# One early product, a few weight buffers and the order of some sums, stores and reads in a hybrid decoder layer

## The chip, the cores and the metric

The kernel runs on one core of one Trainium2 chip. The metric is the device time of one execution in microseconds; the time of a kernel is the median of its runs. The core has five engines with an instruction stream each: TensorE (PE, with its weight loads shown as PEld), VectorE (DVE), ScalarE (ACT), GpSimd (POOL) and SyncE (SP). Each executes its own stream in order. Transfers are issued by the instruction streams, here by SP (its hardware queue) and by POOL (its software queue), and land some microseconds later.

## What is computed

One layer of a hybrid decoder: 1024 tokens and 16 meta tokens, model width 1024, feed-forward width 4096, all float32. The part that matters here is the last line but one:

```python
u = rmsnorm(h, g_pre_mix[l])
z = u @ w_in[l]
...
mix = jnp.concatenate([attn, rec], axis=-1) @ w_out[l]
h = h + rmsnorm(mix, g_post_mix[l])
u = rmsnorm(h, g_pre_ffn[l])
f = jnp.square(jax.nn.relu(u @ w_ff1[l])) @ w_ff2[l]
h = h + rmsnorm(f, g_post_ffn[l])
```

## The kernel before

**Stages.** The in-projection, attention and recurrence take the first 280 us or so, the output projection and its norm run to about 330 us, the first feed-forward matrix (FF1) to about 640 us, the second (FF2) to the end. The change lies in the last stages of the out-projection, in FF1 and in FF2.

**Numbers in two parts.** Every float32 operand is split in a high and a low part (L94 to L101): ACT casts the value (L96) and DVE subtracts the cast from the value (L99). `mm3` (L123) then multiplies high by high (L125), high weights by the low part of the other operand (L126) and low weights by its high part (L127). One `product` (L999) is four of these over the contraction: 12 matmuls of 128x512.

**Seven products in place of eight.** FF1 and FF2 are each worked as a two by two block product in the manner of Strassen: sums of weight blocks times sums of operand blocks, so that seven products do instead of eight, at the price of sums on DVE. FF1 runs over 16 chunks p of 256 columns of `w_ff1`. Its weights come as two loads, r0 (upper half of the contraction) and r1 (lower half). `prep_a(p)` (L1012) issues both, makes the sums in place (four DVE operations of L989), splits what is needed, and stores the summed r1 in `s_dram[p]` on POOL's queue (L1034) for a later loop. The operand sums are t2, t3 and t4; their splits are `ot2`, `ot3`, `ot4`. The splits of t4 are made during the first loop by `t_rest` (L1153) and written to a scratch in DRAM, `t4_dram`, with four stores on SP's queue (L1165), since `ot4` is needed only some 130 us later.

**Buffers.** All slabs come by tag, with a fixed number of buffers each (L55): raw 2, ws 4 (weight splits), a 16, b 17, c 8, d 4, e 2. A load into a buffer waits until its last user is done. r1 of chunks 2 to 5 takes "a" buffers (L1015), which held the projection's splits and later hold results of the chunks; the other chunks take "d".

**Early products.** Before the main loop, while the last tiles of the norm are still worked on, PE computes the products with ready operands: `p1` (L1095) of chunks 0 to 3 and `p2` (L1100) of chunks 0 to 3, `p2` into the PSUM bank "pt", from where DVE adds it to block "11" (L1103). Then the first loop (L1168): for each chunk the second product (with `ot2`, L1173), its copy by ACT (L1174), `p1` of chunk p + 2, and the third product (with `ot3`, L1177), its copy (L1178). Second and third accumulate in the same bank, so the third waits for the copy. For p = 0 there is no `p1` between them, since chunk 2 is done early.

**The second and third loop of FF1.** The second loop (L1197) works the stored sums. Behind it `ot4` is read back from `t4_dram` in four reads on SP's queue (L1214 to L1217): the high halves of both tiles, then the low halves. The third loop runs over the chunks in the order `third` (L1294). Its first step, n = 0, uses `product_by_parts` (L1219), which does the four matmuls high by high, then low weights by high, then high weights by low; so the low halves come into play last. The other steps use `product`.

**FF2.** 56 steps, 7 products by 8 parts (`PLAN`, L1232). `fetch_2` (L1249) loads the weights of a step: one load on SP (L1261), and where a sum of two blocks is wanted, either a second transfer on POOL that adds into the first buffer while landing (L1258, for two of three parts) or a second load, and the sum is made on DVE by `prep_2` (L1270). `prep_2` splits them in "ws" buffers (L1274).

**The order.** Within these dependences a scheduler decides, by simulated times, in which order each engine's stream has its instructions. An extra order without a wait is put in by `behind(name, ins)` (L106): `ins` comes after the instruction of that name in the schedule. `w_low` holds the name of the last low split (L1274); only for i = 6 is the next sum put behind it (L1272).

Of the kernel before, what the change touches and what calls it, by code (L numbers as in the profile page):

```python
# [16 lines left out]
P = 128  # L17
# [20 lines left out]
def hybrid_layer(  # L38
# [6 lines left out]
    nc = tc.nc  # L45
# [23 lines left out]
    def f32(ap):  # L69
        return ap.bitcast(F32)  # L70
# [51 lines left out]

    def mm3(dst, lhs, rhs, start, stop):  # L123
        (lh, ll), (rh, rl) = lhs, rhs
        nc.tensor.matmul(dst, lh, rh, start=start, stop=False, skip_group_check=True)  # L125
        nc.tensor.matmul(dst, lh, rl, start=False, stop=False, skip_group_check=True)  # L126
        last_mm[0] = nc.tensor.matmul(  # L127
            dst, ll, rh, start=False, stop=stop, skip_group_check=True
        ).ins.name
# [868 lines left out]

    def product(acc, w, op, first):  # L999
        wh, wl = w  # L1000
        for kc in range(4):
            hh, ll = op[kc // 2]
            mm3(
                acc, (wh[:, kc, :], wl[:, kc, :]), (hh[:, kc % 2, :], ll[:, kc % 2, :]),
                first and kc == 0, kc == 3,
            )
# [5 lines left out]
    def prep_a(p, late=None):  # L1012
        r0 = slot("raw", [P, 4, 256])
        w1_load(r0, 0, p, 0, 2)
        r1 = slot("a" if 2 <= p < 6 else "d", [P, 4, 256])  # L1015
        w1_load(r1, 1, p, 0, 2)
# [82 lines left out]

    def p2(p, w):  # L1100
        y2 = bank("pt")
        product(y2, w, b21, True)
        nc.vector.tensor_tensor(block("11", p), y2, block("11", p), op=ALU.add)  # L1103
# [41 lines left out]
    a12_early.update(early(1, 2, pair("a", ESH)))  # L1145
    for p in range(2, 4):
        p2(p, a12_early[p])
    ot3 = [pair("b", [P, 2, 512]) for _ in range(2)]
# [5 lines left out]
    def t_rest(k):  # L1154
        i = k % 2
        if k < 2:
            behind(mark[0], combine(u2f[1][i], u2f[1][i], u2f[0][i], ALU.subtract))
        elif k < 4:
            behind(mark[0], combine(t2[i], u2f[0][2 + i], t2[i], ALU.subtract))
        else:  # L1160
            hl = pair("a", [P, 2, 512])
            late = mark[0]
            behind(late, split(*hl, t2[i]))
            for n in range(2):
                nc.sync.dma_start(t4_dram[:, n, 2 * i : 2 * i + 2, :], f32(hl[n]))  # L1165

    raw_b, raw_c = {}, {}
    for p in range(16):  # L1168
# [4 lines left out]
        product(ya[p], wa[p][1], ot2, False)  # L1173
        nc.scalar.copy(block("12", p), ya[p])  # L1174
        if 4 <= p + 2 < 16:
            p1(p + 2, wa[p + 2][0])
# [37 lines left out]
    ot4 = [pair("b", [P, 2, 512]) for _ in range(2)]  # L1214
    for n in range(2):
        for i in range(2):
            nc.sync.dma_start(f32(ot4[i][n]), t4_dram[:, n, 2 * i : 2 * i + 2, :])  # L1217

    def product_by_parts(acc, w, op):  # L1219
        for k, (a, b) in enumerate(((0, 0), (1, 0), (0, 1))):  # L1220
            for kc in range(4):
                nc.tensor.matmul(
                    acc, w[a][:, kc, :], op[kc // 2][b][:, kc % 2, :],
                    start=k == 0 and kc == 0, stop=k == 2 and kc == 3,
                    skip_group_check=True,
                )

# [37 lines left out]
    def prep_2(n, tag="ws"):  # L1265
# [21 lines left out]

    w_low = [None]

# [4 lines left out]
    for n, p in enumerate(third):  # L1294
# [205 lines left out]
```

## Time and the profile before

| What | Value |
|---|---|
| Time, median of 3 runs | 957.42 us (956.74 to 957.98) |
| The profiled execution's own time | 957.43 us |
| Its span | 955.7 us |
| DVE busy | 659.3 us |
| ACT busy | 504.3 us |
| POOL busy | 124.6 us |
| HBM read / written | 109.93 MB / 18.87 MB |
| Loads raw<-w_ff, issue to landing, median | 4.4 us |
| Reads b<-t_dram, issue to landing, median | 5.9 us |

The profile is of one execution. A row of the timeline gives the start, the duration, the engine, the line in the code, the operation, output<-inputs by the program's names (`ps_acc`, `ps_s`, `ps_pt`, `ps_o` are PSUM banks; `ws` and `e` weight splits, `b` operand splits), the shape and, in brackets, how long the engine was idle before it and what ended that. Several like instructions in a row are shown as one, with xN. "SPq" is a transfer at SP's queue; its bar is the issue, the landing comes later. A wait row gives the waiting instruction, the releaser, total, count and longest. A stretch row gives start:end, its length, the busy time with the number of instructions that touch it, the granted clock, the DMA share and GB/s. PE's matmuls overlap, each runs longer than the distance to the next, so that a lost fraction of a microsecond shows as a distance between two starts, and not always as an idle time.

### The profile page before, as it was taken

The numbers are of one execution on the slowest core, as the hardware profiler recorded it, in microseconds if no ns is written. First come the engines' busy times: TensorE is split into PE (matmuls) and PEld (weight loads), VectorE is DVE, ScalarE is ACT, GpSimd is POOL, SyncE is SP. The second block draws the span as 40 slices with busy tenths as digits, with TensorE's granted clock in tenths as the row PEclk, the third lists the DMA queues.
The fourth block names the chain that finished last, engine by engine and source line by source line (L and its number), as shares of the span: only waits on it lengthen the run. The fifth ranks groups of instructions, "written<-read, shape, count | busy, mean of one in ns | idle before, by whom it ended". The sixth has DMA issues, their size and how long they took to land.

```text
span 955.7 us, 12406 instructions
## 1 busy us (share of the span) xinstructions
PE 944.6 (99%) x4728; PEld 789.8 (83%) x4728; DVE 659.3 (69%) x845; ACT 504.3 (53%) x854; POOL 124.6 (13%) x184
## 2 busy tenths in 40 slices
PE   9999999999999999999999999999999999999996
PEld 8999999877888877888888878888888788888885
DVE  6567997779866776665644465476576776779883
ACT  7537766478645554443555575563433343446441
POOL 4102563420020100000000000000111100001201
PEclk9999999999999999999999999999999999999999
DMA  8221011104235466675522353324767765547934
GB/s 271 57 67 23 24 45 46 45 23 134 77 120 177 133 220 198 197 259 160 184 102 90 110 192 119 109 92 129 176 171 182 198 219 178 197 133 199 241 67 89
DMA packets 88200, 130.22 MB, mean 136 GB/s; under 512 B 13702, under 2 KB 52630, under 8 KB 88140
## 3 DMA queue, kind: packets, MB, share of 16 engines
q1 hardware_dynamic: 79548, 106.54, 34.3%
q0 software_dynamic: 8160, 21.57, 10.9%
q10 hardware_dynamic: 432, 1.31, 0.4%
q8 instruction: 37, 0.61, 0.3%
q14 instruction: 23, 0.19, 0.1%
HBM read 109.93 MB, written 18.87 MB: 135 GB/s over the span
## 4 chain that ended last, share of the span: by engine, by line
PE 91%; DVE 3%; ACT 2%; SPq 1%; POOL 1%; DMA 1%; issue 1%; DVEq 0%; ACTq 0%; POOLq 0%
PE ps_acc L125 11%; PE ps_acc L126 11%; PE ps_acc L127 11%; PE ps_pt L125 7%; PE ps_pt L126 7%; PE ps_pt L127 6%; PE ps_s L127 6%; PE ps_s L126 6%; PE ps_s L125 6%; PE ps_o L127 5%; PE ps_o L126 5%; PE ps_o L125 5%; PE ps_o L684 1%; POOL c L673 1%; ACT c L82 1%; DMA c<-in_x_dram 1%
## 5 line engine op out<-in xcount | busy, mean ns | idle before, releaser
L96 ACT CAST ws<-raw 128x1024 fp32r<-128x1024 f32 (+1 forms) x68 | 69.6, 1024 | 121.6 <-PE ps_o L126 46.9
L99 DVE TENSOR_TENSOR ws<-raw,ws 128x1024 fp32r<-128x1024 f32 (+1 forms) x69 | 82.4, 1195 | 53.8 <-ACT ws L96 52.8
L125 PE MATMUL ps_acc<-a,ws 128*128 128x256 f32 (+2 forms) x256 | 85.8, 335 | 0.0
L127 PE MATMUL ps_acc<-a,ws 128*128 128x256 f32 (+2 forms) x256 | 85.2, 333 | 0.0
L126 PE MATMUL ps_acc<-a,ws 128*128 128x256 f32 (+2 forms) x256 | 85.1, 333 | 0.0
L99 DVE TENSOR_TENSOR b<-b,b 128x1024 fp32r<-128x1024 f32 (+2 forms) x50 | 58.9, 1179 | 25.9 <-PE ps_o L126 17.1
L96 ACT CAST ws<-e 128x1024 fp32r<-128x1024 f32 x41 | 42.9, 1046 | 64.0 <-PE ps_o L126 40.2
L96 ACT CAST b<-b 128x1024 fp32r<-128x1024 f32 (+2 forms) x49 | 50.0, 1019 | 45.8 <-DVE b L989 40.2
L99 DVE TENSOR_TENSOR ws<-e,ws 128x1024 fp32r<-128x1024 f32 x41 | 50.1, 1223 | 24.2 <-ACT ws L96 24.0
L673 POOL TENSOR_SCALAR_AFFINE_SELECT c<-c 128x512 fp32r<-128x512 f32 x64 | 52.1, 834 | 70.3 <-ACT c L96 60.8
L125 PEld LDWEIGHTS ps_acc<-a,ws 128*128 128x128 f32 x256 | 48.3, 189 | 4.6 <-issue 0.2
L127 PEld LDWEIGHTS ps_acc<-a,ws 128*128 128x128 f32 x256 | 48.2, 188 | 4.5
L126 PEld LDWEIGHTS ps_acc<-a,ws 128*128 128x128 f32 x256 | 48.1, 188 | 4.4 <-issue 0.4
L126 PE MATMUL ps_acc<-ws,b 128*128 128x512 f32 (+1 forms) x120 | 46.2, 385 | 0.9 <-DVE ws L99 0.9
L125 PE MATMUL ps_acc<-ws,b 128*128 128x512 f32 (+1 forms) x120 | 46.2, 386 | 0.0
L127 PE MATMUL ps_acc<-ws,b 128*128 128x512 f32 (+1 forms) x120 | 46.2, 385 | 0.0
L125 PE MATMUL ps_pt<-ws,b 128*128 128x512 f32 x112 | 44.4, 396 | 0.0
L126 PE MATMUL ps_pt<-ws,b 128*128 128x512 f32 x112 | 44.1, 394 | 0.0
L127 PE MATMUL ps_pt<-ws,b 128*128 128x512 f32 x112 | 44.0, 393 | 0.0
L125 PE MATMUL ps_s<-ws,b 128*128 128x512 f32 x110 | 43.4, 395 | 0.0
L127 PE MATMUL ps_s<-ws,b 128*128 128x512 f32 x110 | 43.3, 394 | 0.0
L126 PE MATMUL ps_s<-ws,b 128*128 128x512 f32 x110 | 43.3, 393 | 0.0
(414 smaller groups left out, 2662.7 us busy)
## 6 DMA issues: line engine op xcount, KB each, us to landing
raw<-in_w_ff_dram SPq DMA_DIRECT2D x61, 512.0 KB, 4.4
e<-in_w_ff_dram SPq DMA_DIRECT2D x45, 512.0 KB, 3.4
d<-in_w_ff_dram SPq DMA_DIRECT2D x12, 512.0 KB
s_dram<-d POOLq DMA_DIRECT2D x12, 512.0 KB, 4.1
c<-in_x_dram SPq DMA_DIRECT2D x8, 512.0 KB, 3.5
raw<-in_w_in_dram SPq DMA_DIRECT2D x8, 512.0 KB
d<-in_x_dram SPq DMA_DIRECT2D x8, 512.0 KB, 3.2
out_dram<-raw SPq DMA_DIRECT2D x8, 512.0 KB
```

What stands on the lines that cost most here:

```text
L82: ins = nc.scalar.activation(*args, **kwargs).ins
L96: nc.scalar.copy(hi, src)
L99: low = nc.vector.tensor_tensor(lo, src, f32(hi), op=ALU.subtract).ins
L125: nc.tensor.matmul(dst, lh, rh, start=start, stop=False, skip_group_check=True)
L126: nc.tensor.matmul(dst, lh, rl, start=False, stop=False, skip_group_check=True)
L127: last_mm[0] = nc.tensor.matmul(dst, ll, rh, start=False, stop=stop, skip_group_check=True).ins.name
L673: nc.gpsimd.affine_select(out=p_[:, :, s], in_=f32(p_[:, :, 0]), pattern=[[0, 4], [g, P]], compare_op=op, fill=0.0, base=0, channel_multip ...
L684: nc.tensor.matmul(po[:, oc : oc + n], v, p_[:, pc : pc + n], start=first and k == 0, stop=last and k == 1, skip_group_check=True,)
```

## The change

It has five parts.

- `p2` of chunk 3 moves from the early products into the first loop, for p = 0, between the copy of the second product and the third product. A new argument `after` puts its first matmul behind the last matmul of the second product.
- r1 of chunks 2 to 13, not 2 to 5, takes "a" buffers.
- The four stores to `t4_dram` go out on POOL's queue.
- `ot4` is read tile by tile (high and low of the first, then of the second), and the step n = 0 uses `product` like the others.
- In FF2 the sum of step n, for i < 6 and n > 1, is put behind the low split of step n − 2.

With them the scheduler arrives at other orders. On DVE they differ between about 340 and 460 us and between 675 and 760 us: a low split of weights comes ahead of the sum of a later step, and in FF1 the sum for chunk 14 comes ahead of the low split of chunk 13. On POOL and SP four pairs of adding transfers and loads of FF2 are exchanged, and the loads of r1 of chunks 14 and 15 go out right after that of chunk 6. On PE only `p2` of chunk 3 changes its place and the 12 matmuls of the step n = 0 change their order.

```diff
-    def mm3(dst, lhs, rhs, start, stop):
+    def mm3(dst, lhs, rhs, start, stop, after=None):
         (lh, ll), (rh, rl) = lhs, rhs
-        nc.tensor.matmul(dst, lh, rh, start=start, stop=False, skip_group_check=True)
+        ins = nc.tensor.matmul(
+            dst, lh, rh, start=start, stop=False, skip_group_check=True
+        ).ins
+        if after:
+            behind(after, ins)
...
-    def product(acc, w, op, first):
+    def product(acc, w, op, first, after=None):
...
-                first and kc == 0, kc == 3,
+                first and kc == 0, kc == 3, after if kc == 0 else None,
...
-        r1 = slot("a" if 2 <= p < 6 else "d", [P, 4, 256])
+        r1 = slot("a" if 2 <= p < 14 else "d", [P, 4, 256])
...
-    def p2(p, w):
+    def p2(p, w, after=None):
         y2 = bank("pt")
-        product(y2, w, b21, True)
+        product(y2, w, b21, True, after)
...
-    for p in range(2, 4):
-        p2(p, a12_early[p])
+    p2(2, a12_early[2])
...
-                nc.sync.dma_start(t4_dram[:, n, 2 * i : 2 * i + 2, :], f32(hl[n]))
+                nc.gpsimd.dma_start(t4_dram[:, n, 2 * i : 2 * i + 2, :], f32(hl[n]))
...
         nc.scalar.copy(block("12", p), ya[p])
+        if p == 0:
+            p2(3, a12_early[3], last_mm[0])
...
-    for n in range(2):
-        for i in range(2):
+    for i in range(2):
+        for n in range(2):
             nc.sync.dma_start(f32(ot4[i][n]), t4_dram[:, n, 2 * i : 2 * i + 2, :])
...
             ins = combine(raws[0], raws[0], raws[1], wx[2])
             if i == 6:
                 behind(w_low[0], ins)
+            elif n > 1:
+                behind(w_lows[n - 2], ins)
         wh, wl = pair(tag, [P, 2, 512])
-        w_low[0] = split(wh, wl, raws[0]).name
+        w_low[0] = w_lows[n] = split(wh, wl, raws[0]).name
...
-        if n == 0:
-            product_by_parts(y4, wc[p][1], ot4)
-        else:
-            product(y4, wc[p][1], ot4, True)
+        product(y4, wc[p][1], ot4, True)
```

More of the change, by code (lines that the diff above doesn't have):

```diff
@@ L1214, in hybrid_layer @@
     ot4 = [pair("b", [P, 2, 512]) for _ in range(2)]
-    for n in range(2):
-        for i in range(2):
+    for i in range(2):
+        for n in range(2):
             nc.sync.dma_start(f32(ot4[i][n]), t4_dram[:, n, 2 * i : 2 * i + 2, :])
[L1219 to L1226, printed above, removed]
     w2v = w_ff2.rearrange("(q s a p) (b c) -> q a b p s c", s=2, a=2, p=P, b=2)
@@ L1286, in hybrid_layer @@
     ready, raw_2 = {}, {}
-    w_low = [None]
+    w_low, w_lows = [None], {}
     load_root(squared)
```

## The prediction

> **What bounds the kernel now.** I began with the page's head, for the span and the busy shares, then read what TensorE (PE) and its weight loads (PEld) waited for, and then PE's busy time in stretches.
>
> ```profile
> span 955.7 us, 12406 instructions
> PE 944.6 (99%) x4728; PEld 789.8 (83%) x4728; DVE 659.3 (69%) x845; ACT 504.3 (53%) x854; POOL 124.6 (13%) x184
> ...
> PE ps_acc L303 <- DVE base_e L557: 1.5, 1, 1.5
> ...
> 341.00:367.00 26.00, 25.32 (x107) 1.00 0.63 207
> 367.00:559.00 192.00, 192.00 (x829) 1.00 0.49 162
> 559.00:564.00 5.00, 5.00 (x22) 1.00 0.72 248
> 564.00:741.00 177.00, 177.00 (x766) 1.00 0.51 139
> 741.00:744.00 3.00, 2.06 (x10) 1.00 0.36 110
> 744.00:942.00 198.00, 198.00 (x885) 1.00 0.59 171
> ```
>
> PE is the bound: 944.6 of 955.7 us, at a granted clock of 1.00 in all six stretches. The long stretches give its pace: 192.00 us over 829 matmuls is 0.2316 us from start to start. The change adds and removes no matmul, so it can move the end only by opening or closing gaps in that row. The largest wait, 1.5 us on base_e, belongs to L303 and L557, in the attention part, which the change leaves alone. Of the 601 us from 341 to 942, PE idles in two stretches only, 26.00 − 25.32 = 0.68 us and 3.00 − 2.06 = 0.94 us; some smaller losses, in which a matmul starts late without an idle row, come below. **All there is to win is some 3 us, 0.3% of the time**; 0.2%, about what a measurement of this kernel can tell from no change, is 1.9 us. VectorE (DVE, 69%) and the DMA queues matter where one result is late.
>
> **Part A: the last early product is moved (p2 of chunk 3, 12 matmuls).**
>
> ```profile
> 341.34 0.40 PE L126 MATMUL ps_pt<-b,a 128*128 128x512 f32 x1
> ...
> 346.66 0.40 PE L127 MATMUL ps_acc<-b,e 128*128 128x512 f32 x1
> 347.73 0.50 PE L125 MATMUL ps_acc<-b,ws 128*128 128x512 f32 x1 [0.68 <-ACT a L1174]
> 348.07 0.39 PE L126 MATMUL ps_acc<-b,ws 128*128 128x512 f32 x1
> ...
> 362.24 0.39 PE L126 MATMUL ps_s<-b,e 128*128 128x512 f32 x1
> 362.53 0.51 PE L127 MATMUL ps_s<-b,e 128*128 128x512 f32 x1
> ...
> 340.65 0.76 DVE L99 TENSOR_TENSOR b<-a,b 128x256 fp32r<-128x256 f32 x2 [0.33 <-ACT b L96]
> 350.99 1.29 DVE L99 TENSOR_TENSOR e<-raw,e 128x512 fp32r<-128x512 f32 x2
> 357.80 0.69 DVE L989 TENSOR_TENSOR a<-raw,a 128x512 f32<-128x512 f32 x1 [4.92 <-DMA raw<-in_w_ff_dram]
> ```
>
> The second product of chunk 0 (L1173) ends with the matmul that starts at 346.66. The third (L1177) reuses its PSUM bank and waits for the copy of L1174 until 347.73; the next matmul starts at 348.07. Two steps of 0.23 took 1.41 us, so the stall costs 1.41 − 0.46 = 0.95. After the change the 12 matmuls of p2(3), 12 × 0.2316 = 2.8 us, stand between the two, and a copy of 0.6 us hides behind them. The second product then starts where p2(3) stood, at about 341.4. It needs its operand's last low half at its eighth matmul, near 343.0; the low splits that started at 340.65 are over by 341.4 (0.76 us for two), or 342.6 if DVE does the sum of p2(2) ahead of the last: in time. The third product starts near 346.9 instead of 347.73.
>
> What is late next? In the same stretch four smaller starts are late, each read in the same manner from pairs of rows such as 362.24 and 362.53 (0.29 instead of 0.23, with a long next step): near 350.7, 351.7, 362.5 and 365.5, together about 0.7. The stretch's row agrees: of its 107 matmuls two only reach in at its ends (each runs 0.39, 0.23 apart), and 26.00 − 105 × 0.2316 = 1.7 = 0.95 + 0.7. They wait for splits of weight sums. In front of those, PE comes 0.95 earlier, and DVE, rid of the p2(3) sum at this place, 0.6 earlier: the low split at 350.99 stays just in time, and I leave 0.4 of loss there. The two late starts at 362 and 365 come from the chunk whose load DVE awaited until 357.80; that load goes out with a buffer freed sooner, and I take those two as closed. A: 0.95 + 0.7 − 0.4, rounded, **a gain of 1.2** (bounds 0 and 1.65).
>
> **Parts B and C: r1 of chunks 6 to 13 in "a" buffers.** The buffers hold nothing else then, so no load waits for them. But "d" becomes free for chunks 14 and 15, whose loads the SP queue issues far ahead, and DVE's order changes with it.
>
> ```profile
> 362.51 0.37 SPq L986 DMA_DIRECT2D raw<-in_w_ff_dram  x1
> 367.44 0.68 DVE L99 TENSOR_TENSOR e<-raw,e 128x512 fp32r<-128x512 f32 x1
> a<-in_w_ff_dram SPq DMA_DIRECT2D x4, 512.0 KB, 7.3
> ...
> 432.72 0.69 DVE L989 TENSOR_TENSOR d<-raw,d 128x512 f32<-128x512 f32 x1 [1.19 <-DMA d<-in_w_ff_dram]
> 435.14 0.69 DVE L99 TENSOR_TENSOR e<-raw,e 128x512 fp32r<-128x512 f32 x1
> 438.65 1.23 DVE L99 TENSOR_TENSOR ws<-raw,ws 128x1024 fp32r<-128x1024 f32 x1 [2.83 <-ACT ws L96]
> ...
> 440.82 0.39 PE L127 MATMUL ps_acc<-b,ws 128*128 128x512 f32 x1
> DMA to landing us min/median/max: 5.7/5.7/5.7
> ```
>
> B: the load of chunk 5's r1, which in the old order was long there, now goes out with its r0, as the second of five in a row, near 361.8 (the r0 load at 362.51, about 0.8 earlier with PE). DVE sums it ahead of the low split that stood at 367.44, and PE needs that split about 370.0. The "a" loads took 7.3 us as a median, which gives 369.1 plus four operations, 371.5: 1.5 late. A landing after 5 us gives 369.2, in time. It is second of the burst, and the r0 at its side is nearer to 5: I take 0.3 lost (bounds 0 and 1.5).
>
> C: near 438, DVE's sum for chunk 14, which stood after it before, now comes ahead of chunk 13's low split (438.65), and must wait for chunk 14's r0. That load follows the low split of 435.14, which itself moves up by some 1.6 us (it no longer stands behind all four sums that began with the wait of 432.72), less what PE gains: out at 434.2. With the 5.7 us that two raw loads of this stretch took, it lands at 439.9, the sum ends at 440.6 and the split at 441.9, where PE wants it at 440.82: 1.05 lost. If it lands before 437.9 the split isn't late at all. Half: **0.5 lost**.
>
> **The t4 stores on POOL's queue.** Four issues leave SP and stand between POOL's stores of L1034. Nothing waits for them before the ot4 reads over 100 us later, nor does PE wait for those stores. Price 0; were the cover gone, one POOL issue would cost about half a microsecond.
>
> ```profile
> 435.62 0.53 POOL L1034 DMA_DIRECT2D s_dram<-d  x1 [10.02 <-DVE d L989]
> 559.94 3.21 PE L1222 MATMUL ps_pt<-b,ws 128*128 128x512 f32 x12
> 562.41 0.30 PEld L1222 LDWEIGHTS ps_pt<-b,ws 128*128 128x128 f32 x2 [0.43 <-DMA b<-t_dram]
> 552.95 2.85 SPq L1217 DMA_DIRECT2D b<-t_dram  x4
> ```
>
> **Part D: ot4 in plain product order.** The four reads start at 552.95. Before, the step begins at 559.94 with eight matmuls on the operand's high halves; the fourth read, the low half of the second tile, is needed by the 11th, at 559.94 + 10 × 0.2316 = 562.25, and PE resumes at 562.41, with about 0.28 lost in all. The plain product meets the low part of its second tile, the fourth read in the new order too, at its eighth matmul: 561.56. 562.41 − 561.56 = 0.85, and 0.1 for a slow restart: 0.95 instead of 0.28, **0.7 lost** (bounds 0 and 0.9).
>
> [...]
>
> **Parts E and F: the second weights.** In FF2 the sum of a step now stands behind the low split of two steps before.
>
> ```profile
> 740.51 1.23 DVE L989 TENSOR_TENSOR e<-e,raw 128x1024 f32<-128x1024 f32 x1 [2.77 <-DMA raw<-in_w_ff_dram]
> 741.65 1.22 DVE L99 TENSOR_TENSOR ws<-e,ws 128x1024 fp32r<-128x1024 f32 x1
> 741.59 0.40 PE L125 MATMUL ps_o<-ws,b 128*128 128x512 f32 x1
> 742.93 0.50 PE L126 MATMUL ps_acc<-ws,b 128*128 128x512 f32 x1 [0.94 <-DVE ws L99]
> 743.26 0.39 PE L127 MATMUL ps_acc<-ws,b 128*128 128x512 f32 x1
> ...
> 726.33 1.21 POOL L1258 DMA_DIRECT2D e<-in_w_ff_dram  x1 [6.47 <-DMA e<-in_w_ff_dram]
> 732.03 1.21 POOL L1258 DMA_DIRECT2D raw<-in_w_ff_dram  x1 [4.50 <-DVE b L99]
> DMA to landing us min/median/max: 5.4/5.7/9.4
> ```
>
> E: the split PE waits for stood in DVE's queue behind a sum that waited 2.77 us for a load. From 741.59 to 743.26 PE took 1.67 for two steps of 0.23: 1.2 lost. Put ahead of the sum, the split needs only its own weights. Their adding transfer (L1258), however, is now the second of its pair: 732.03 instead of 726.33, landing 5.7 later at 737.7; the cast of 1.05 us and the split of 1.22 give 740.0, and PE wants it at 741.8. **A gain of 1.2** (bounds 0 and 1.2).
>
> F: the next pair, before at 745.81 and 752.75 on POOL, is exchanged too, so the weights that came at 752 come at about 756; with cast and split, 758.4, against a need of 758.5 once PE runs 1.2 earlier. I take 0.3 lost (bounds 0 and 0.8). The other exchanges of this kind, and the copies that ACT does ahead of a cast, shift by at most one operation (a cast 1.05, a split 1.23) with results that lie longer than that before their use.
>
> **Sum**, against the profiled execution of 957.43 (its span and 1.7 around it; the median is 957.42): − 1.2 + 0.3 + 0.5 + 0 + 0.7 − 1.2 + 0.3 = − 0.6, so **956.8 us**, no change that can be told.
>
> **The rivals.** (1) *Faster, 954.6.* Nothing new comes late: A whole (1.65), E (1.2), B, C, D and F nothing; 957.43 − 2.85. For it: DVE has 31% idle and most loads are far ahead. Against it: the rows of D have the read at 562.41. (2) *Slower, 959.5.* The in-order wait of C. Chunk 14's load takes as long as the slowest of the raw loads, 8.05:
>
> ```profile
> DMA to landing us min/median/max: 3.0/4.5/8.1
> ```
>
> then it lands at 434.2 + 8.05 = 442.25, sum and split end at 444.2, PE stands 3.4 us and 0.1: 956.8 − 0.5 + 3.5 = 959.8, or 959.5 where PE, late already by B or F, wants it 0.3 later. It decides from a landing at 441.3 on, 7 us after issue. Against it: 5.7 in this stretch. (3) *The change doesn't do what it says, 958.0.* The wait for the copy goes, but PE runs into weight splits that were 0.95 from being late all along (350.99 is such a row), so A gives nothing: 956.8 + 1.2.
>
> **How the numbers follow.** Forecast 0.42; A without gain 0.20; faster 0.14; slower 0.24, as it holds B, C and F, each in the same direction and each with an end of about 1 us. "Same" is within 1.9 of 957.42, 955.5 to 959.3: the forecast and rival 3, 0.62. The range, 955.2 to 959.6, reaches so far to both rivals that about a tenth is left out on each side: 955.2 lies a third of a microsecond below where A and E come whole and one of the losses of D's size stays (957.42 − 2.85 + 0.95 = 955.5), 959.6 at the in-order wait. The likeliest case's own is 955.8 to 957.8, one unknown term of 1 us either way.
>
> **What would show it.** Right: no wait on the L1174 copy, and 12 ps_pt matmuls between the second and third product near 344; no DVE wait on ws near 742; a PE wait on the t_dram read near 561 of 0.8 or more. Wrong: a DVE wait for raw near 438 with PE waiting on ws after it (C large); PE waits on e near 350 or 370 above 0.5; a POOL landing later than 740 in the pair that began at 726. Any new PE wait above 2 us would overturn the forecast.

## The result, and the profile after

The changed kernel takes 970.56 us as a median of 4 runs (968.68 to 971.15), the kernel before 957.36 beside it: a ratio of 1.0134, with a 95% interval of 1.0117 to 1.0152. The forecast was 956.8 with a range of 955.2 to 959.6. The change costs 13 us, where the forecast's slower rival had 2.

From the page's head and the list of PE's waits, after:

```profile
span 968.9 us, 12415 instructions
PE 948.6 (98%) x4728; PEld 791.2 (82%) x4728; DVE 658.5 (68%) x845; ACT 503.8 (52%) x854; POOL 127.3 (13%) x188
...
PE ps_acc L125 <- ACT ws L96: 5.9, 3, 3.0
PE ps_acc L131 <- DVE ws L99: 2.7, 1, 2.7
PE ps_pt L130 <- DMA b<-t_dram: 1.8, 2, 1.2
```

The wait for the copy of L1174 is gone, and so is the wait on DVE's ws split near 742. In their place stand three waits on an ACT cast of weights, one on a low split and two on the reads of t4. The line numbers of the code have moved by some four, up or down (mm3's three matmuls are L125, L130 and L131 now, the adding transfers of FF2 L1254, the loads L1257). PE's busy time in stretches shows where (start:end, length, busy time with the matmuls that touch it, granted clock, DMA share, GB/s):

```profile
341.00:367.00 26.00, 25.94 (x112) 1.00 0.66 212
...
438.00:447.00 9.00, 6.25 (x20) 0.81 0.21 59
...
562.00:568.00 6.00, 4.12 (x16) 1.00 0.85 310
...
718.00:728.00 10.00, 7.03 (x23) 0.83 0.76 150
728.00:773.00 45.00, 41.97 (x179) 1.00 0.70 163
```

The first stretch holds 112 matmuls where it held 107, and the long stretches left out are all busy at a clock of 1.00. The loss lies in the four others shown, two of them with a granted clock of 0.81 and 0.83 (the last section says what stands behind these). The account, each number the distance between two starts in PE's timeline less the usual 0.23:

| Place, us | lost before | lost after | difference |
|---|---|---|---|
| 346 to 367, first chunks | 1.65 | 0.4 | −1.2 |
| 438 to 446, chunk 13's weights | 0 | 4.6 | +4.6 |
| 562 to 567, ot4 | 0.3 | 2.7 | +2.4 |
| 718 to 726, FF2 | 0 | 5.0 | +5.0 |
| 741 to 743 before, 751 to 754 after | 1.2 | 1.6 | +0.4 |
| 769 to 773, FF2 | 0 | 2.6 | +2.6 |
| sum | | | +13.8 |

The spans differ by 13.2; the profile after was 0.4 ahead of the other at 341 us, where the first moved matmul stands.

PE's timeline of the changed kernel at the places that count:

```profile
346.25 0.39 PE L131 MATMUL ps_pt<-b,a 128*128 128x512 f32 x1
346.48 0.39 PE L125 MATMUL ps_acc<-b,ws 128*128 128x512 f32 x1
...
438.99 0.40 PE L130 MATMUL ps_acc<-b,ws 128*128 128x512 f32 x1
442.13 0.50 PE L131 MATMUL ps_acc<-b,ws 128*128 128x512 f32 x1 [2.75 <-DVE ws L99]
...
442.94 0.62 PE L131 MATMUL ps_acc<-b,ws 128*128 128x512 f32 x1
443.36 0.63 PE L125 MATMUL ps_acc<-b,ws 128*128 128x512 f32 x1
...
562.93 0.40 PE L125 MATMUL ps_pt<-b,ws 128*128 128x512 f32 x1
564.49 0.50 PE L130 MATMUL ps_pt<-b,ws 128*128 128x512 f32 x1 [1.16 <-DMA b<-t_dram]
...
718.45 0.40 PE L131 MATMUL ps_o<-ws,b 128*128 128x512 f32 x1
721.80 0.50 PE L125 MATMUL ps_acc<-ws,b 128*128 128x512 f32 x1 [2.95 <-ACT ws L96]
```

At 346.25 the last matmul of p2(3) is followed by the third product 0.23 later: part A did what was forecast, and the 0.4 that it left is at 350.5, at the split where the forecast had it. At 438.99 PE meets a split that ends 2.9 late, and a little after it the matmuls start 0.43 apart, not 0.23, and last 0.63: eight of them cost another 1.6. The same happens behind the stall at 718.45. At 562.93 the plain product meets its second read at its second matmul, and it isn't there.

**Where the split at 438 was.** DVE's timeline:

```profile
435.12 0.68 DVE L993 TENSOR_TENSOR raw<-raw 128x512 f32<-128x512 f32 x1
440.25 0.69 DVE L993 TENSOR_TENSOR d<-raw,d 128x512 f32<-128x512 f32 x1 [4.45 <-DMA raw<-in_w_ff_dram]
440.86 1.22 DVE L99 TENSOR_TENSOR ws<-raw,ws 128x1024 fp32r<-128x1024 f32 x1
```

The split of 440.86 stands behind chunk 14's sum, which waited 4.45 us for chunk 14's upper load. This is the in-order wait of the forecast's second rival, with the load in at 440.2. It went out at 435.23 on SP's queue, 5.0 us before.

**Where the cast at 718 was.** The chain runs back through POOL and DVE; the changed kernel first, then the kernel before:

```profile
692.41 1.23 POOL L1254 DMA_DIRECT2D e<-in_w_ff_dram  x1 [5.03 <-DVE b L993]
701.20 1.23 DVE L99 TENSOR_TENSOR ws<-e,ws 128x1024 fp32r<-128x1024 f32 x1 [3.55 <-ACT ws L96]
702.34 1.22 DVE L993 TENSOR_TENSOR e<-e,raw 128x1024 f32<-128x1024 f32 x1
706.70 1.20 POOL L1254 DMA_DIRECT2D e<-in_w_ff_dram  x1 [13.06 <-DMA e<-in_w_ff_dram]
714.95 1.22 POOL L1254 DMA_DIRECT2D raw<-in_w_ff_dram  x1 [7.05 <-DVE b L99]
720.70 1.04 ACT L96 CAST ws<-raw 128x1024 fp32r<-128x1024 f32 x1 [9.57 <-DMA raw<-in_w_ff_dram]
```

```profile
693.50 1.23 DVE L989 TENSOR_TENSOR e<-e,raw 128x1024 f32<-128x1024 f32 x1 [4.79 <-DMA raw<-in_w_ff_dram]
...
698.91 1.21 POOL L1258 DMA_DIRECT2D raw<-in_w_ff_dram  x1 [11.37 <-DVE b L99]
```

Read the first of them upwards. The cast at 720.70 waits for the adding transfer issued at 714.95. Before, that transfer (raw) was the first of its pair, at 698.91, and is now the second, 16 us later, of which 5.5 are the kernel's delay by then. It is second because the sum of step 13 (693.50 before, 702.34 now) stands behind the low split of step 11 (701.20), and the load into the raw buffer that this sum frees goes out behind it. And that split is late because its own weights were the second of the pair before: issued at 692.41, landed at 700.1, where the cast took them up.

**Where part E's gain went.** The wait on the split is gone there, but now the cast of the same weights is late:

```profile
745.69 1.22 POOL L1254 DMA_DIRECT2D e<-in_w_ff_dram  x1 [6.45 <-issue]
751.58 1.04 ACT L96 CAST ws<-e 128x1024 fp32r<-128x1024 f32 x1 [7.63 <-DMA e<-in_w_ff_dram]
```

PE would have wanted this cast's result at 751.55 and its next matmul started at 752.67. The weights are second of their pair, as forecast, but go out 7.65 us behind the first (738.04) where the distance was 5.70 in the kernel before (726.33 and 732.03).

### The profile page after: what moved, and what is told of

Its sections match the earlier page's. It is cut to its first block, busy times and chain, and to the rows that moved or that the text cites. A ratio compares the mean times of both kernels' runs of the same rounds, so it can differ in the third digit from the quotient of the medians.

```text
span 968.9 us, 12415 instructions
## 1 busy us (share of the span) xinstructions
PE 948.6 (98%) x4728; PEld 791.2 (82%) x4728; DVE 658.5 (68%) x845; ACT 503.8 (52%) x854; POOL 127.3 (13%) x188
## 4 chain that ended last, share of the span: by engine, by line
PE 83%; DMA 7%; DVE 6%; issue 2%; POOL 1%; ACT 1%; SPq 0%; DVEq 0%; ACTq 0%; POOLq 0%
PE ps_acc L131 10%; PE ps_acc L130 10%; PE ps_acc L125 10%; PE ps_pt L130 6%; PE ps_pt L131 6%; PE ps_pt L125 6%; PE ps_s L131 5%; PE ps_s L130 5%; PE ps_s L125 5%; PE ps_o L130 5%; PE ps_o L125 5%; PE ps_o L131 5%; DMA raw<-in_w_ff_dram 3%; PE ps_o L688 1%; DMA a<-in_w_ff_dram 1%
## 5 line engine op out<-in xcount | busy, mean ns | idle before, releaser
L125 PE MATMUL ps_acc<-a,ws 128*128 128x256 f32 (+2 forms) x256 | 85.8, 335 | 0.0
L131 PE MATMUL ps_acc<-a,ws 128*128 128x256 f32 (+2 forms) x256 | 85.2, 333 | 0.0
L130 PE MATMUL ps_acc<-a,ws 128*128 128x256 f32 (+2 forms) x256 | 85.1, 333 | 0.0
L125 PE MATMUL ps_acc<-ws,b 128*128 128x512 f32 (+1 forms) x120 | 46.8, 391 | 5.9 <-ACT ws L96 5.9
L125 PEld LDWEIGHTS ps_acc<-a,ws 128*128 128x128 f32 x256 | 48.3, 189 | 4.6 <-issue 0.2
L131 PEld LDWEIGHTS ps_acc<-a,ws 128*128 128x128 f32 x256 | 48.2, 188 | 4.5
L130 PEld LDWEIGHTS ps_acc<-a,ws 128*128 128x128 f32 x256 | 48.1, 188 | 4.5 <-issue 0.4
L130 PE MATMUL ps_acc<-ws,b 128*128 128x512 f32 (+1 forms) x120 | 47.0, 392 | 0.1
L131 PE MATMUL ps_acc<-ws,b 128*128 128x512 f32 (+1 forms) x120 | 46.5, 388 | 0.0
L125 PE MATMUL ps_pt<-ws,b 128*128 128x512 f32 x112 | 44.3, 395 | 0.0
L130 PE MATMUL ps_pt<-ws,b 128*128 128x512 f32 x112 | 44.1, 394 | 0.0
L131 PE MATMUL ps_pt<-ws,b 128*128 128x512 f32 x112 | 44.0, 393 | 0.0
L130 PE MATMUL ps_s<-ws,b 128*128 128x512 f32 x110 | 43.5, 395 | 0.0
L125 PE MATMUL ps_s<-ws,b 128*128 128x512 f32 x110 | 43.5, 395 | 0.0
L131 PE MATMUL ps_s<-ws,b 128*128 128x512 f32 x110 | 43.4, 395 | 0.0
```

Of the source, the lines that this page charges most:

```text
L125: ins = nc.tensor.matmul(dst, lh, rh, start=start, stop=False, skip_group_check=True).ins
L131: last_mm[0] = nc.tensor.matmul(dst, ll, rh, start=False, stop=stop, skip_group_check=True).ins.name
```

## The experiments

Each kernel was run beside the kernel before on its chip; ratios are to that. Interval in brackets: 95%.

### One part undone in the changed kernel

**Without the fifth part.**

```diff
             if i == 6:
                 behind(w_low[0], ins)
-            elif n > 1:
-                behind(w_lows[n - 2], ins)
```

> The changed kernel without its fifth part: in FF2 no sum is put behind an earlier low split, all else as changed. Theory: this part costs about 8 us. PE's start times against the kernel before grow by 5.0 at 718 us (a 3.1 us stall, then matmuls at half pace), 0.35 net at 741 to 751 and 2.6 at 769, because the pairs of adding transfers of L1254, which land one behind the other, are exchanged and the late one is the one needed. Without it: 970.6 - 8 = 962.6, no wait on ACT's ws cast behind 700 us, and the old stall of 1.2 us near 741 back. Rival: the part gives its 1.2 us as predicted and FF2 is late because everything ahead of it has shifted the loads; then 970.6 + 1.2 = 971.8, with the waits at 718 and 769 still there.

958.7 against 958.69: ratio 1.001 (0.9991 to 1.0029). The theory holds as to the part that costs the time, and the rival falls. The number is 3.9 us under the 962.6 given for it, as the loss near 438 is small in the profiled run. PE's waits of this run:

```profile
PE ps_pt L130 <- DMA b<-t_dram: 1.9, 2, 1.1
...
PE ps_acc L130 <- DVE ws L99: 0.7, 1, 0.7
...
PE ps_acc L131 <- DVE ws L99: 0.3, 1, 0.3
```

No wait on a cast is left. The wait near 438 is 0.3 here, with the same order on DVE: its size is a matter of when the load lands. The reads of t4 are as late as before. The old stall near 742 did not come back in this run; a smaller one of the same kind lies at 761.

**DVE's order near 438 put back.**

```diff
-            wa[p + 2] = prep_a(p + 2, None if p else urgent)
+            wa[p + 2] = prep_a(p + 2, mark_ws[0] if p == 12 else None if p else urgent)
...
-            split(hi, lo, r0)
+            mark_ws[0] = split(hi, lo, r0).name
```

> The changed kernel, with the sums of chunk 14 put behind the low split of chunk 13 again; the buffers and loads stay as changed, and on DVE alone the order differs, near 435 to 455 us. Theory: PE's 4.6 us of loss at 438.7 (2.9 idle, 0.1, 1.6 for eight matmuls at half pace) come from DVE's in-order wait for chunk 14's load, so the time falls by 4.6 to 966.0 and the half-pace matmuls there go too. Rival: the hoisted loads of chunks 14 and 15 make the load of chunk 13 or 14 late, whatever DVE's order is; then the time stays at 970.6 within 1, with a PE wait near 438 or one chunk later.

965.48, ratio 1.0083 (1.0058 to 1.0109), with 971.2 for the profiled run and 964.8 to 966.1 for the others. DVE's timeline of the profiled run:

```profile
437.06 1.23 DVE L99 TENSOR_TENSOR ws<-raw,ws 128x1024 fp32r<-128x1024 f32 x1 [1.56 <-ACT ws L96]
...
448.06 0.69 DVE L993 TENSOR_TENSOR d<-raw,d 128x512 f32<-128x512 f32 x1 [4.93 <-DMA raw<-in_w_ff_dram]
...
449.40 1.22 DVE L99 TENSOR_TENSOR ws<-raw,ws 128x1024 fp32r<-128x1024 f32 x1
```

The split of chunk 13 is in time, at 437.06. But the edit let the scheduler put the sum of chunk 15 (448.06) ahead of the split of chunk 14 (449.40), so the same in-order wait stands one chunk later, and PE waits 2.93 us there, again with half pace behind it. The rival's number and place fit this profiled run, the theory's number the other three. The rows decide for the theory as to the cause: each split that is late stands behind a sum that waits for a load. The kernel of e7, below, fits this: up to FF2 its loads have the changed kernel's order, both sums have their old places, and PE waits neither near 438 nor near 450 in its profile. The price of the stall near 438 alone was not separated by this run.

**The fourth part undone.**

```diff
-    for i in range(2):
-        for n in range(2):
+    for n in range(2):
+        for i in range(2):
             nc.sync.dma_start(f32(ot4[i][n]), t4_dram[:, n, 2 * i : 2 * i + 2, :])
...
+        if n == 0:
+            product_by_parts(y4, wc[p][1], ot4)
+        else:
             product(y4, wc[p][1], ot4, True)
```

> The changed kernel with its fourth part undone: the reads of ot4 in the old order and the step n = 0 by parts (high by high, low weights by high, high weights by low). Theory: the reads land late by 1.8 us against the kernel before (the second read 8.5 us behind the first issue), and the plain product meets the second one at its second matmul; by parts it is the third and fourth read that matter, behind eight matmuls, so that of the 2.5 us lost at 562 to 567 some 1.0 to 1.5 stay: 969.0 to 969.6. Rival: the slow landing comes from the order of the reads, so that both go: 968.1. Second rival: it makes no difference, 970.6.

965.61, ratio 1.0085 (1.0062 to 1.0108). In its profile nothing waits near 438 either, so the time is not to be compared with 970.6 directly; at the place itself 0.4 us are lost in place of 2.7. The first rival, that the order of the reads makes them late, looked better than the theory, and was tried by itself below.

### The parts one at a time in the kernel before

**The first part alone** (p2 of chunk 3 moved, as in the diff of the change).

> The kernel before with the first part of the change alone: p2 of chunk 3 between the second and the third product of chunk 0. Theory: the 1.2 us that PE's start times show between 346 and 367 us are kept to the end: 957.4 - 1.2 = 956.2. Rival: a later wait takes it back, as for a load whose buffer comes free no earlier: 957.4.

961.59 against 958.69: ratio 1.0026 (1.0012 to 1.004). Slower, and neither theory nor rival had that. The stall of the copy is gone, but the profile has others, near 412, 424 and 450:

```profile
409.66 0.69 DVE L993 TENSOR_TENSOR d<-raw,d 128x512 f32<-128x512 f32 x1 [3.67 <-DMA d<-in_w_ff_dram]
...
447.73 0.69 DVE L993 TENSOR_TENSOR d<-raw,d 128x512 f32<-128x512 f32 x1 [4.97 <-DMA d<-in_w_ff_dram]
...
PE ps_s L125 <- ACT ws L96: 1.2, 1, 1.2
PE ps_s L131 <- DVE ws L99: 1.0, 2, 0.5
```

DVE waits for lower loads into "d" buffers, of which there are four: a load waits until a sum is stored to s_dram and landed. PE is 1.2 earlier, those loads aren't. In the changed kernel the second part takes this wait away. How much of the 0.26% this explains is open: the profiled run, 959.13, was the fastest of the twelve, the scheduler also moved DVE's sums between 341 and 383 us, and the stall near 450 is not the first part's alone. It stands in profiles of kernels with PE at its old time there (2.9 us lost in e5, 1.9 in e11), and was absent from the kernel before's own.

**The second part alone**, with the sums of chunks 14 and 15 kept behind the splits of chunks 13 and 14 (the edit of e2 with `p >= 12`).

> The kernel before with the second part alone, DVE's sums of chunks 14 and 15 kept behind the low splits of chunks 13 and 14. Theory: the stalls of 0.5 to 3.5 us near 448, which differ from run to run in the kernel before, wait for chunk 14's lower load, which waits for a d buffer; with that load long there they go: 0.5 to 1.5 us less as a median, and a spread of the runs of 2 to 3 us instead of 5. Rival: the a buffers alone win nothing, 0.999 to 1.001, and what the first, second and third part won together (ratio 0.998) is the first part's 1.2 us.

957.98 against 957.12: ratio 1.0008 (1.0000 to 1.0017). The rival holds: by itself it wins nothing. Its profile has no stall near 450, as the theory had it, but one of 1.5 us near 424. The spread of its 11 runs is 2.2 us (957.01 to 959.21); that of the kernel before was 3.7 there, but over 24 runs.

**First, second and third part together**, orders as in e15, ot4 as before, no fifth part.

> The changed kernel with the first, second and third part only (p2 of chunk 3 moved, r1 of chunks 2 to 13 in the a buffers, t4 stores on POOL), ot4 read and used by parts as before, no order of the fifth part, and on DVE the sums of chunks 14 and 15 behind the low splits of chunks 13 and 14 as before. Theory: what the first part gains (1.2 us between 346 and 367) is kept, as no d buffer is waited for now, and no stall takes its place: 1.0 to 1.5 us under the kernel before, ratio 0.9984 to 0.9990. Rival: a load between 370 and 450 is late for the earlier PE, as in the first part alone, and the ratio is 1.000 to 1.003.

956.03 against 957.96: **ratio 0.998 (0.9970 to 0.9989), faster than both kernels.** The first two parts go together: 1.0026 and 1.0008 apart, 0.998 together. That they need each other is likely, not shown, as the t4 stores on POOL's queue came with them and weren't tried alone.

**The same with the order of step 21 added.**

> The same with one order of the fifth part, that of step 21 alone: the low split of step 19 ahead of the sum that waited for a load near 740 us. Theory: the stall of up to 1.2 us near 742 goes and nothing else comes, as the next adding transfers have slack of some 1 us: 0.5 to 1.2 us under the run without it. Rival: the exchange of the next pair (before at 746 and 753) makes the weights wanted at 758.5 late by 1 us or more and the gain is eaten or turned round.

956.21, ratio 0.9988 (0.9976 to 1.0000), beside 956.03 without: no difference that can be told, where the theory had a gain of 0.5 to 1.2. The stall near 742 is not there with it, but it wasn't there in e7's profile either, and a loss of 0.6 us stands at 758.6, where the forecast's part F had one.

**The order of the reads alone** (the two `for` lines of e3, in the other direction, in the kernel before).

> The kernel before with one change: the four reads of ot4 tile by tile, as in the changed kernel; the step by parts stays, so nothing else differs in any engine's order. Theory: in this order the reads land 1 to 2 us later (second read some 8 us behind the first issue instead of 6, fourth 11 instead of 9.4), and the step by parts, which wants the third read at its third matmul, stands about 2 to 3 us: plus 1.5 to 3 us with at most 0.3 at that place before. Rival: the reads land as before and only their order counts: the third read, 7.7 behind the first issue, is wanted at 7.5: plus 0.2 to 0.4.

961.06 against 957.92: ratio 1.0028 (1.0011 to 1.0046). The only edit is the order of two reads, and no engine's order differs by it. Issue to landing, from the view of that line, in this kernel, and PE's wait; then the first of these in e9, which reads in the old order and ran on the same chip. The trace has a landing for one of the four reads only, the second issued, which is why the three numbers of a view are one:

```profile
DMA to landing us min/median/max: 7.8/7.8/7.8
...
PE ps_pt L1222 <- DMA b<-t_dram: 1.9, 1, 1.9
```

```profile
DMA to landing us min/median/max: 6.4/6.4/6.4
```

In the kernel before it was 5.9 (the table ahead of the prediction has it as a median of the reads; it is this one read), and 5.9 to 6.4 in all ten profiles that have it in the old order. So the second read lands 1.4 to 1.9 later. The others are seen where PE waits for them: it got on with the fourth 9.5 us behind the first issue in the kernel before and 11.2 in the changed kernel, and with the third at 9.6 here. The theory holds: tile by tile the reads land later, on top of being wanted in another order. Why, no run here shows. Not all of this run's time is theirs: of the profile, 1.9 us were lost near 450, too.

### The orders of the fifth part

The steps 10, 13, 18 and 21 are those of its orders that exchange a pair of transfers; a fifth sum, near 755, moves on DVE alone. Each kernel has `elif n == 13:` or the like in place of `elif n > 1:`, in the kernel before.

**Step 13 alone, step 10 alone.**

> The kernel before, with one single order of the fifth part: in FF2 the sum of step 13 (e<-e,raw near 693 us) behind the low split of step 11. On DVE only this sum moves behind that split, and on SP and POOL only the next pair of loads and adding transfers changes places. Theory: the split must wait for its ws buffers, which PE frees some 8 us later, so the sum, the load into the raw buffer that it frees and the adding transfer into it all go out about 8 us later and behind the other of the pair; its weights land near 714, PE wants their cast at 712.5, a stall of 1 to 3 us at 713, with matmuls at half pace behind it if the stall nears 3: plus 1.5 to 5 us. Rival: the loss needs the exchange of the pair before (step 10), which made the split of step 11 late; then this order alone costs under 0.5 us.

> The kernel before, with the order of step 10 alone: the low split of step 8 ahead of the sum of step 10 near 677 us, and the pair of loads and adding transfers of steps 11 and 12 exchanged. Theory: step 11's weights land one adding transfer, 6 to 8 us, later, near 692 to 694, and PE wants them at 696, so nothing waits: same as before within 0.5 us. Rival: this is where the loss of FF2 begins; then PE waits on a ws cast at 696 or 713 and the time grows by 2 us or more.

957.76 and 957.74 against 957.96: ratios 0.9998 (0.9987 to 1.0010) and 0.9998 (0.9987 to 1.0009). Neither costs anything; for step 13 the rival holds, for step 10 the theory.

**Both.**

> The kernel before with the orders of steps 10 and 13 of the fifth part together, which alone cost nothing each. Theory: the two add up to a chain. The exchange at step 10 lets step 11's weights land last of their pair, so the low split of step 11 is late; the sum of step 13 stands behind that split, and the loads into the buffers that both free, and the two adding transfers behind them, start some 4 us later than with the order of step 13 alone, where the weights landed at 713 just in time. PE waits 3 us or more near 713 to 718 for an ACT cast, with matmuls at half pace behind it: 4 to 5.5 us over the kernel before. Rival: the chain needs the orders of steps 18 and 21 too, or the earlier parts of the change; then the time is the same within 0.5 us.

962.29 against 957.92: ratio 1.0040 (1.0024 to 1.0056). The theory holds, the rival falls, and PE's timeline has the stall of the changed kernel, with half pace behind it:

```profile
713.38 0.40 PE L127 MATMUL ps_o<-ws,b 128*128 128x512 f32 x1
716.84 0.50 PE L125 MATMUL ps_acc<-ws,b 128*128 128x512 f32 x1 [3.07 <-ACT ws L96]
...
719.12 0.63 PE L125 MATMUL ps_acc<-ws,b 128*128 128x512 f32 x1
```

Zero and zero make four: on POOL the step 13 pair goes out at 701.27 and 709.95 here and the cast waits for the second of them, the chain read above.

**Steps 18 and 21.**

> The kernel before with the orders of steps 18 and 21 alone. Theory: they are a chain of their own, as those of steps 10 and 13 were: the pair near 726 is exchanged, so step 19's weights land second, the low split of step 19 is late, the sum of step 21 stands behind it, and the loads and the adding transfers of the pair near 746 with it; PE waits 1 to 1.5 us near 745 and 2 to 3 us near 760, and the old stall of up to 1.6 us near 742 is gone: plus 2 to 5 us. Rival: these stalls come only where the chain of steps 10 and 13 has set everything back; then 0 to minus 1.2.

959.31 against 957.12: ratio 1.0027 (1.0013 to 1.0040), 2.2 us. A chain of its own, as the theory had it, with a PE wait on the cast of 2.1 us near 760; of the stall that it gave near 745, 0.3 us came.

**All orders, nothing else.**

> The kernel before with the whole fifth part and nothing else. Theory: the two chains add up, with the stalls near 713, 746 and 763 of the changed kernel: plus 7 to 10 us, ratio 1.007 to 1.011. Rival: the chains need the earlier PE of the first part to be felt in full; then under 5.

960.12 against 957.12: ratio 1.0043 (1.0023 to 1.0062), less than theory, and what the rival gave. So it was run again, between the changed kernel and the changed kernel without these orders:

> The changed kernel beside e17 and e18 on one chip. Theory: the orders of FF2 cost more in the changed kernel than alone (e14: ratio 1.0043), because the earlier parts bring more adding transfers to 7 us and more instead of 5.4: 1.010 to 1.014 here. Rival: the chip decides how long these transfers take; then the difference between this and e17 is that of e14, 0.003 to 0.006.

> The changed kernel without its fifth part, beside e16: 0.999 to 1.002, as in the first run of it; e16 less this is the price of the fifth part inside the change, 8 to 12 us by the theory, 3 to 6 by the rival.

> The fifth part alone in the kernel before, beside e16: 1.003 to 1.006 by the theory, as in e14 (958 to 961 us). By the rival it is as far above the kernel before as e16 is above e17.

| | median, us | ratio to before (957.83) |
|---|---|---|
| e16, the changed kernel | 969.31 | 1.0114 (1.0089 to 1.0139) |
| e17, without the fifth part | 958.55 | 1.0012 (0.9993 to 1.0032) |
| e18, the fifth part alone | 965.86 | 1.0093 (1.0064 to 1.0123) |

Here the fifth part alone costs 8.0 us, not 3.0, and inside the change 969.31 − 958.55 = 10.8. Issue to landing of the adding transfers, first in e14's profile, then in e18's:

```profile
DMA to landing us min/median/max: 5.4/5.6/9.0
```

```profile
DMA to landing us min/median/max: 5.6/6.8/9.1
```

The same program cost 3.0 us on one chip and 8.0 on another, and the intervals just don't meet (1.0023 to 1.0062, 1.0064 to 1.0123). So the chain doesn't need the earlier parts of the change, against the theory of e16 and the rival of e14; whether these add to it (10.8 against 8.0, intervals of some 3 us each way) stays open. What differs is how long the adding transfers take: their median is 1.2 us longer, and the first of the step 13 pair landed 5.6 us after its issue in e14 and 7.2 in e18, with the second behind it. PE's waits on ACT's casts of weights came to 1.4 us in e14's profile and to 4.2 in e18's; that the longer transfers add up to this along the chain is the likely reading. That the chip is the reason is not shown. Each view is of one run, one of e14's seven runs took 966.33, and on a single chip the medians went from 5.9 to 7.4 over the kernels tried there.

### Two more

**The changed kernel again.**

> The changed kernel once more, beside the others on one chip. Theory: two kinds of run, by whether chunk 14's load lands before DVE needs it near 438: with a stall there 968 to 971, without 964 to 966; the FF2 stalls near 718, 751 and 769 are in both. Rival: the stall near 438 is always there and only its size varies, 968 to 971 throughout.

967.75 against 957.92: ratio 1.0120 (1.0081 to 1.0159). Three runs at 967.4 to 968.1, one at 973.0. In the profiled run (967.42) DVE's sum of chunk 14 starts at 437.64, after a wait of 3.79, where PE lost 0.1 us, so the stall near 438 is not always there, as the theory had it. The three lie 1.4 to 2.1 us above its 964 to 966; the FF2 stalls of the profiled one were larger than those of the first (the longest 3.4 in place of 3.0). What the run of 973.0 lost is not on record; that it is the kind with the stall is a guess from its time.

**A ladder of stalls.**

```diff
             split(hi, lo, r0)
+            for _ in range({5: 2, 7: 3, 9: 3, 11: 4}.get(p, 0)):
+                nc.vector.tensor_tensor(lo, r0, f32(hi), op=ALU.subtract)
```

> The kernel before, where the low split of the weights of chunks 5, 7, 9 and 11 is done again 2, 3, 3 and 4 times over itself on DVE (1.23 us each), so that PE meets late weights by 1 to 4 us at four places. Theory: a stall under about 2 us costs itself and 0.1; from one of 3 us on some eight matmuls follow at 0.427 us from start to start instead of 0.231, 1.6 us more. Rival: the half pace in the changed kernel has another cause than the length of the stall; then it comes at none of the places, or at all.

977.56 in the single run. PE's stalls came out at up to 1.6 us (usual pace behind them), and at 4.2 and 6.5 (half pace, for seven and thirteen matmuls). The theory holds as far as it was tried; the sizes between were not hit here, but in other runs, and there the length of a stall is not what decides (the last section).

## Why the forecast was wrong, by its steps

- **What bounds the kernel, and the ceiling of the gain:** right. PE's busy time grew by 4.0 us with the same 4728 matmuls, most of it the half pace behind two stalls, and nothing tried won more than 0.2%.
- **A (gain 1.2):** right inside the changed kernel, to the tenth and in its mechanism. That this gain is only kept if the next loads are as early was not in the working: alone, the part lost 0.26% (e4).
- **B (loss 0.3):** no late split near 370; the first five loads came in time.
- **C (loss 0.5):** the mechanism and the place were right; the term was mis-sized, by 4.1 us. The load landed at 440.2 and the split ended at 442.1, where the forecast had 439.9 and 441.9. But PE wanted the split at 439.2. The forecast held the old 440.82 against it, though by its own part A PE comes about a microsecond earlier; that alone makes the bound of 1.05 some 2. Most of the rest is the 0.4 by which this execution was ahead, the half that was taken of the bound, and 1.6 for eight matmuls at half pace, which had no place in the sum. In the profiles of the same order it measured 0 (e3), 0.1 (e10), 0.5 (e1, e16), 3.0 (e17) and 4.6. The small ones have the load out at 433.0 to 434.0 and in 4.0 to 4.4 us later, the two large ones 435.2 and 5.0 to 5.3. The forecast gave it a half of a bound, where it is a thing with two ends.
- **D (loss 0.7):** the mechanism was right and the size off: 2.4 more than before, and 1.7 to 2.8 us lost at the place in all six profiles that have this part. The step took the landing times of the old order of reads (562.41 for the fourth) for the new one. They are part of what the order changes (e11): here PE met the second read first, 8.5 us behind the first issue, and the fourth at 11.2.
- **The t4 stores on POOL (0):** no run shows a wait for them; not tried alone.
- **E and F (gain 1.2, loss 0.3), and the exchanges priced at nothing:** this is the step that failed. "The other exchanges of this kind, and the copies that ACT does ahead of a cast, shift by at most one operation (a cast 1.05, a split 1.23) with results that lie longer than that before their use": the pair at 680.57 and 686.33 on POOL and the pair at 698.91 and 704.71 are two of these, and the sentence prices each against the times of the kernel before. One by one they do cost nothing (e5, e6). Together they cost 4.4 us (e9), and 5.0 in the changed kernel, since the second starts from what the first made late. What the forecast had as a shift of one operation was a sum put behind a split that waits for its weights, which moved from 693.50 to 702.34. E and F fail in the same way, as their transfers were given the old distance within a pair. In place of a gain of 1.2 the place of E lost 0.4 more than before, and F lost 2.6 in place of 0.3. FF2 so cost 8.0 us where the sum had a gain of 0.9, and that is 8.9 of the 14.4 us between the table's sum and the forecast's (C is 4.1, D 1.7, B and rounding the rest). The stall near 742 is not a fixed thing either: it is 0 to 1.7 us in the profiles of kernels that have the old order there.
- **The rivals.** The slower one, by the in-order wait of C, was right in kind and had 0.24; its 959.5 needed the load 7 us after issue, while 5 were enough, as PE came 1.6 us before the time that it reckoned with. The largest loss was in none of the rivals. A stall of 3 us that costs half as much again wasn't thought of.

## What to carry to other kernels

Where one engine is at 99%, an order that takes away a wait of 1 us is read for what it puts the waiting instruction behind: follow each reordered pair through to the next one with the shifted times, not with the old ones, as long as one's release is the other's start. An in-order engine must not have an instruction that waits for a transfer ahead of one that the bound engine needs, however early the transfer seems to be: DVE's sum at 440.25 waited 4.45 us for its load, and the split behind it ended at 442.1, where PE wanted it at 439.2. And two edits that are neutral or worse apart can be worth having together (e4, e15, e7): an engine that comes earlier has to find its loads earlier.

## What the runs showed of the hardware

**Half pace after a stall.** After some stalls PE's matmuls follow at 0.427 us from start to start, not 0.231, for 3 to 6 us (442.94 to 446.34 in the changed kernel, 418.09 to 423.80 in the ladder). A stall's length alone doesn't decide. At the same place, with the same order up to there, an idle time of 2.75 in the changed kernel had half pace behind it (the rows above), and one of 2.78 in e17 had none, while in e18 1.76 us were enough:

```profile
442.34 0.50 PE L131 MATMUL ps_acc<-b,ws 128*128 128x512 f32 x1 [2.78 <-DVE ws L99]
```

```profile
715.10 0.50 PE L125 MATMUL ps_acc<-ws,b 128*128 128x512 f32 x1 [1.76 <-ACT ws L96]
```

It came after idle times of 1.76 (e18), 1.94 (e3, at 765.06), 2.75 and 2.95 (the changed kernel), 2.93 (e2), 3.07 (e9) and 6.32 (the ladder), and not after 2.02 (the changed kernel, at 771.97) and 2.78 (e17). Where it lasts six to eight matmuls it costs some 1.2 to 1.6 us, six to eight times 0.427 − 0.231.

In the rows below it goes by how the stall lies on a grid in time. The granted clock in the profiles of the kernel before and the changed kernel is 1.00 or 0.50, and within each of the two it changes only at times that lie whole steps of 3.413 us apart. In the changed kernel it falls at 442.93 and at 722.82, which is 82 such steps, and rises again one step after each; in the kernel before its one stretch at 1.00 runs from 7.10 to 952.59, 277 steps. Stretches of one step, in the changed kernel, in e17 and in e18 (length, PE's busy time, clock):

```profile
439.52:442.93 3.41, 0.80 (x3) 1.00 0.00 1
442.93:446.35 3.42, 3.42 (x10) 0.50 0.25 77
```

```profile
440.58:443.99 3.41, 1.65 (x7) 1.00 0.00 0
443.99:447.41 3.42, 3.42 (x17) 1.00 0.52 139
```

```profile
712.50:715.91 3.41, 1.65 (x8) 1.00 0.02 4
715.91:719.32 3.41, 3.41 (x9) 0.50 1.02 150
```

In the changed kernel 2.61 us of the idle time lie in one step, and the next step has the half clock. In e17 a boundary of the grid cuts the 2.78 in two, of 1.02 and 1.76, and nothing follows. In e18 the whole 1.76 lie in one step, and the next has the half clock. At 1.76 us of idle PE within a step it went both ways. In the changed kernel the step from 719.40, with 2.39 us of idle PE, had the half clock behind it too, and the one from 770.60, with 1.42, had not.

The grid lies differently from run to run: the boundaries shown for e17 (440.58, 443.99) lie 1.06 us behind those of the changed kernel (439.52, 442.93). In the step ahead of the half clock PE was still busy for 0.80 us in the changed kernel (439.52) and for 1.65 in e18 (712.50). What sets the grid, no run here shows.

**Transfers differ in length from run to run of the same code.** The adding transfers' median was 5.6 to 7.4 us over these profiles (5.6 in e14 and 6.8 in e18, one program), and the second of four reads took 1.4 to 1.9 us longer in another order of the reads.
